# Six plain up-projections, sums in ten steps, and two products' pools exchanged, in a hybrid decoder's inference step

## The chip, the cores and the metric

The kernel runs on one core of a Trainium2 chip. A core has a matrix engine (TensorE, with its weight loads listed apart as PEld), a vector engine (VectorE, DVE in the trace), an activation engine (ScalarE, ACT), a general engine (GpSimd, POOL) and queues that start DMA transfers (SyncE, SP). Each engine executes its own instructions in a fixed order and waits on semaphores for the others. The metric is the device time of one launch in microseconds; less is better. Executions of the same kernel differ by some tenths of a per cent.

## The reference

Two layers (DEPTH = 2) of a decoder trunk are applied to 1024 prompt tokens and to 8 x 4 sample tokens. In each layer three kinds of heads mix the tokens, a projection and a layer norm follow, and then a gated convolutional feed-forward part, the one that the change touches:

```python
def _conv_ffn(x, conv0, w_up, conv_w, conv_b, w_down):
    t_ = x.shape[1]
    u = x @ w_up
    buf = jnp.concatenate([conv0.astype(u.dtype), u], axis=1)
    c = conv_b + sum(conv_w[j] * buf[:, j:j + t_] for j in range(CONV_W))
    a, b = jnp.split(c, 2, axis=-1)
    return (jax.nn.gelu(a) * b) @ w_down, buf[:, -(CONV_W - 1):]
...
        f, cv = _conv_ffn(x, s_conv[l], ffn_up[l], ffn_conv_w[l], ffn_conv_b[l], ffn_down[l])
        x = _layer_norm(ALPHA * x + f, ln2_g[l], ln2_b[l])
```

D_MODEL is 1024, D_FF 2816, CONV_W 3; everything is float32.

## The kernel before

Activations lie with channels on the 128 partitions and tokens along the free axis. The 1056 tokens are cut into three blocks n = 0, 1, 2 of 384, 384 and 288 columns; block 2 holds the 32 sample tokens first. To keep float32 accuracy in fast matmuls every operand is split into a high and a low part (`split`: a cast on ScalarE, the difference on GpSimd, or on VectorE where said), and each product is three matmuls: high x high, high x low and low x high (`mm3`, recorded at line 140).

The feed-forward part runs over NJ = 22 steps j, one for 128 gate channels and the 128 value channels that belong to them. A step makes the two up-projections u (8 k-tiles of 128 input channels each), the three-tap convolution (`conv_start`, line 1437, on ScalarE, then `taps`, line 1433, on VectorE), the gate (`up_gate`: GELU on ScalarE, the product on VectorE at line 1467, then the split), and hands the result to the down-projection. Steps are taken in pairs (j, j + 1). In the middle of step j the function `between` runs the down-projection of the pair before, `downs(j - 2, ...)`: for two halves, three blocks and four output tiles, 24 groups of six matmuls, each group into one PSUM tile, which VectorE then adds to an accumulator `acc[n][m]` in SBUF. The third argument `group` of `downs` counts the pairs: 0 for the first. In group 0 the accumulator isn't read but set, and the residual ALPHA * x goes in, with its high part first (it frees the PSUM tile) and its low part after it: two VectorE instructions per group of matmuls (line 1664). In later groups it is one addition (line 1660).

There are two ways to make a step. `up_first` (step 0) and `up_plain` (steps 1 to 3) multiply directly: per half i of the step (gate, value) and block n, 8 k-tiles x 3 matmuls. `up` (steps 4 to 21) treats blocks 0 and 1, the two halves of the channels and the two halves of k as a 2 x 2 product in Winograd's form: seven products of four k-tiles for eight (into tiles named pa, pg, pb, pc, pf, pd and pe), with weight sums s1 to s4 made on VectorE (lines 1602 to 1605) and sums of activations q1 to q4; block 2 is done directly there, in tiles p0 and p1 (both `p` in the trace). The results are put together on VectorE with additions from PSUM (lines 1596, 1610, 1616, 1617, 1623, 1624, 1633).

The sums of activations q1 to q4 must exist before step 4. The generator `sums` makes them, split into high and low parts: for each of four k-tiles t3 = x1[1] upper minus lower quarter (differences on GpSimd), then t2 and t4 (differences on VectorE), eight VectorE and five GpSimd instructions per k. Last come the differences that overwrite the lower quarter of x1[1] in place, on GpSimd for even k and VectorE for odd. Differences live in buffers d that share a ring of six (tag `u`) with the up-projections. `up_plain` calls `then(j, i, n)` after each group, and where that place stands in `times`, the generator does its next piece: one k after each of the first four places, the whole in-place part after the fifth.

PSUM has eight tiles of a bank: three in pool `pg`, five in pool `pd`. Plain groups take `pd` tiles for n = 0, 1 and `pg` tiles for n = 2 (`bank`); in `up` p0, p1 and the second product (p2, named pg) are in `pg`, the others and all down groups in `pd`. A tile that is taken again makes TensorE wait until its last reader is done.

The order of TensorE is the order in which the program writes the matmuls. The other engines' orders come from the compiler's scheduler, which goes by program order and by the times of a simulated run, so an instruction can be moved ahead of one that is not ready in that simulation. On the chip each engine then keeps that order.

Of the kernel before, what the change touches and what calls it, by code (L numbers as in the profile page):

```python
# [10 lines left out]
F32 = mybir.dt.float32  # L11
# [3 lines left out]
ALU = mybir.AluOpType  # L15
# [3 lines left out]
P = 128  # L19
# [11 lines left out]
ALPHA = (2 * DEPTH) ** 0.25  # L31
# [138 lines left out]
def step_kernel(ctx: ExitStack, tc: tile.TileContext, xT, wA, wB, wO, wU, wD, pp, pb, lora, bg, bgk, shT, cvT, srw, sgl, srt,  # L170
# [12 lines left out]
    pg = pool("pg", 3, PSUM)  # L183
# [137 lines left out]
    for l in range(depth):  # L321
# [1151 lines left out]
        def sums():  # L1473


            (h0, l0, _), (h1, l1, _) = x1[:2]
            t2, t3, t4 = ([jp.tile([P, 4, 384], F32R, tag="tq", name=f"{n}{p}", bufs=6) for p in "hl"] for n in ("t2", "t3", "t4"))

            def x(n, k):
                return [t[:, k].bitcast(F32) for t in x1[n][:2]]  # L1480

            qs = [(h0[:, 0:4], l0[:, 0:4]), (h0[:, 4:8], l0[:, 4:8]), (h1[:, 4:8], l1[:, 4:8]), (h1[:, 0:4], l1[:, 0:4]), t2, t3, t4]
            yield qs

            def new():
                return fp.tile([P, 386], F32, tag="u", name="d", bufs=6)[:, 0:384]

            def two(h, lo, raw, e):
                A.copy(h, raw)
                e.tensor_tensor(lo, raw, h.bitcast(F32), ALU.subtract)  # L1490

            def apart(e, a, b):

                d, f = new(), new()
                e.tensor_tensor(d, a[0], b[0], ALU.subtract)
                e.tensor_tensor(f, a[1], b[1], ALU.subtract)
                e.tensor_tensor(d, d, f, ALU.add)
                return d

            def minus(e, a, d):  # L1500

                e.tensor_tensor(d, a[0], d, ALU.subtract)
                e.tensor_tensor(d, d, a[1], ALU.add)
            for k in range(4):
                d = apart(G, x(1, k + 4), x(1, k))
                two(t3[0][:, k], t3[1][:, k], d, G)
                d = apart(V, x(1, k), x(0, k))
                minus(V, x(1, k + 4), d)
                two(t2[0][:, k], t2[1][:, k], d, G)
                f = new()  # L1510
                V.tensor_tensor(f, x(0, k + 4)[0], d, ALU.subtract)
                V.tensor_tensor(f, f, x(0, k + 4)[1], ALU.add)
                two(t4[0][:, k], t4[1][:, k], f, V)
                yield
            for k in range(4):
                d = apart(V if k % 2 else G, x(1, k), x(0, k))
                two(h1[:, k], l1[:, k], d, V)
            yield

        def product(ps, w, x, first=True, last=True):  # L1520

# [3 lines left out]
        def bank(n, name):  # L1525
            return (pg.tile([P, 512], F32, tag="g", name=name) if n == 2 else pd.tile([P, 512], F32, tag="d", name=name))[:, :NB[n][1]]
# [30 lines left out]
        def up_plain(j, between, then):  # L1557

            hs, cs = [], []
            for i in range(2):  # L1560
                t = j + i * NJ
                w, prev = [whole(wu(t, half), f"wU{t}") for half in range(2)], None
                for n in range(3):
                    c, prev = plain(t, i, n, w, prev)
                    cs.append(c)
                    if i:
                        hs.append(up_gate((cs[n], c), n))
                    then(j, i, n)
                if i == 0:
                    between()  # L1570
            return hs

        def up(j, qs, late=False, between=lambda: None):


            b11, b21, b22, q1, q2, q3, q4 = qs
            t0, t1 = j, j + NJ
            x2 = [(x1[2][0][:, 0:4], x1[2][1][:, 0:4]), (x1[2][0][:, 4:8], x1[2][1][:, 4:8])]
            r11, r12, r21, r22 = (raw_piece(wu(t, half), f"wU{t}") for t in (t0, t1) for half in range(2))
            pa = bank(0, "pa")  # L1580
            w = piece(r11, "a11")
            product(pa, w, b11)
            u22 = new_u()
            A.copy(u22[:, 2:386], pa)
            if not late:
                p0, p1 = bank(2, "p0"), bank(2, "p1")
                product(p0, w, x2[0], True, False)
            w = piece(r12, "a12")
            if not late:
                product(p0, w, x2[1], False, True)  # L1590
                c20, u20 = conv_samples(t0, 0, p0)
            p2 = pg.tile([P, 512], F32, tag="g", name="pg")[:, :384]
            product(p2, w, b21)
            u11 = new_u()
            v11, v22 = u11[:, 2:386], u22[:, 2:386]
            V.tensor_tensor(v11, v22, p2, ALU.add)
            c11 = conv_prompt(t0, 0, u11, v11, True)
            if not late:
                product(p1, piece(r21, "a21"), x2[0], True, False)

            s1 = wf.tile([P, 512], F32, tag="wr", name="s1r", bufs=FR)
            V.tensor_tensor(s1, r21, r22, ALU.add)
            V.tensor_tensor(r21, r11, r21, ALU.subtract)
            V.tensor_tensor(r11, s1, r11, ALU.subtract)
            V.tensor_tensor(r12, r12, r11, ALU.subtract)
            pb_ = bank(0, "pb")
            product(pb_, piece(r11, "s2"), q2)
            u12 = new_u()
            v12 = u12[:, 2:386]
            V.tensor_tensor(v12, v22, pb_, ALU.add)  # L1610
            between()
            p5 = bank(0, "pc")
            product(p5, piece(s1, "s1"), q1)
            p7 = bank(0, "pf")
            product(p7, piece(r21, "s3"), q3)
            V.tensor_tensor(v22, v12, p7, ALU.add)
            V.tensor_tensor(v12, v12, p5, ALU.add)
            p4 = bank(0, "pd")
            w = piece(r22, "a22")
            product(p4, w, q4)  # L1620
            u21 = new_u()
            v21 = u21[:, 2:386]
            V.tensor_tensor(v21, v22, p4, ALU.add)
            V.tensor_tensor(v22, v22, p5, ALU.add)
            halo(u22, 1, u21)
            hs = [up_gate((c11, conv_prompt(t1, 1, u21, v21, True)), 0)]
            if not late:
                product(p1, w, x2[1], False, True)
                c21, u2 = conv_samples(t1, 1, p1)
                conv_rest(t1, c21, u2, u22)  # L1630
            p3 = bank(0, "pe")
            product(p3, piece(r12, "s4"), b22)
            V.tensor_tensor(v12, v12, p3, ALU.add)  # L1633
            halo(u12, 1, u11)
            c12 = conv_prompt(t0, 0, u12, v12)
            hs.append(up_gate((c12, conv_prompt(t1, 1, u22, v22)), 1))
            if late:
                for t, half, p in ((t0, 0, 0), (t0, 1, 0), (t1, 0, 1), (t1, 1, 1)):
                    if half == 0:
                        ps = bank(2, f"pu{t}")  # L1640
                    product(ps, whole(wu(t, half), f"wU{t}"), x2[half], half == 0, half == 1)
                    if half:
                        c, u = conv_samples(t, p, ps)
                        conv_rest(t, c, u, (u12, u22)[p])
                        if p:
                            c21 = c
                        else:
                            c20 = c
            else:
                conv_rest(t0, c20, u20, u12)  # L1650
            hs.append(up_gate((c20, c21), 2))
            return hs

        def down(m, n, group, hs, ws):
            ps = pd.tile([P, 512], F32, tag="d", name="pd")[:, :NB[n][1]]
            for i, (h, w) in enumerate(zip(hs, ws)):
                mm3(ps, *w, *h[n], i == 0, i == len(hs) - 1)
            a = acc[n][m]
            if group:
                V.tensor_tensor(a, a, ps, ALU.add)  # L1660
            else:

                for x, y in zip(x1[n][:2], (ps, a)):
                    V.scalar_tensor_tensor(a, x[:, m].bitcast(F32), ALPHA, y, ALU.mult, ALU.add)

        def downs(j, hs, group):
            for half in range(2):
# [5 lines left out]

        make = sums()
        qs = next(make)
        times = ((1, 0, 2), (1, 1, 2), (2, 0, 2), (2, 1, 2), (3, 1, 1))

        def then(*at):
            if at in times:
# [2 lines left out]
        for j in range(0, NJ - 2, 2):  # L1682

            def between():
                if j:
                    downs(j - 2, hs, j // 2 - 1)
            if j == 0:
                a = up_first()
            elif j < 4:
                a = up_plain(j, between, then)  # L1690
            else:
                a = up(j, qs, between=between)
            hs = [a, up(j + 1, qs) if j >= 4 else up_plain(j + 1, lambda: None, then)]

        xs = [None] * 3

# [213 lines left out]
```

## Time and profile before

| | us |
|---|---|
| median of 3 runs (lowest, highest) | 3405.08 (3397.25, 3408.31) |
| the profiled execution's own time | 3395.68 |
| its span, first to last instruction | 3393.9 |

The mean granted TensorE clock of the profiled execution is 0.945 of full speed. Layer 0's feed-forward part takes about 883 to 1660 us of the span, layer 1's about 2580 to 3370 us. In the profile's rows a line is that of the kernel or of a helper, `out<-in` names the tiles, a bracket gives the idle time before an instruction and what ended it, and a matmul's duration (0.34 us for 384 columns) overlaps the next one's, so that the distance of starts is what counts. A few records of matmuls can be missing.

### The profile page before, as it was taken

The numbers are of one execution on the slowest core, as the hardware profiler recorded it, in microseconds if no ns is written. First come the engines' busy times: TensorE is split into PE (matmuls) and PEld (weight loads), VectorE is DVE, ScalarE is ACT, GpSimd is POOL, SyncE is SP. The second block draws the span as 40 slices with busy tenths as digits, with TensorE's granted clock in tenths as the row PEclk, the third lists the DMA queues.
The fourth block names the chain that finished last, engine by engine and source line by source line (L and its number), as shares of the span: only waits on it lengthen the run. The fifth ranks groups of instructions, "written<-read, shape, count | busy, mean of one in ns | idle before, by whom it ended". The sixth has DMA issues, their size and how long they took to land. (4 is left out here: it accounts for less than half of the span.)

```text
span 3393.9 us, 59056 instructions
## 1 busy us (share of the span) xinstructions
PE 3103.4 (91%) x21618; PEld 2868.3 (85%) x21618; DVE 2374.4 (70%) x5085; ACT 1577.6 (46%) x3635; POOL 1575.1 (46%) x1512
## 2 busy tenths in 40 slices
PE   8889999998889999999788899998998899999995
PEld 8778887777889999999687787876778899999994
DVE  3586764566797777777857667644667977777778
ACT  6754432654534334434586534325545334344346
POOL 5542222144655555545675422221346555455556
PEclk9989999988999999999898899998989899999997
DMA  7443223443301111111264432233433011111111
GB/s 242 147 130 83 70 68 121 120 131 104 90 26 44 56 43 46 47 54 54 96 193 142 115 78 68 65 118 113 129 114 90 25 44 54 41 51 47 54 53 66
DMA packets 245566, 291.14 MB, mean 86 GB/s; under 512 B 76620, under 2 KB 158316, under 8 KB 245276
## 3 DMA queue, kind: packets, MB, share of 16 engines
q1 hardware_dynamic: 225004, 274.08, 26.8%
q10 hardware_dynamic: 20272, 13.29, 1.6%
q8 instruction: 170, 2.79, 0.3%
q14 instruction: 120, 0.98, 0.1%
HBM read 228.85 MB, written 58.43 MB: 85 GB/s over the span
## 5 line engine op out<-in xcount | busy, mean ns | idle before, releaser
L1433 DVE SCALAR_TENSOR_TENSOR c<-u,ppt,c 128x32 f32<-128x32 f32 (+3 forms) x704 | 514.2, 762 | 71.3 <-ACT c L1437 65.9
L197 POOL TENSOR_TENSOR wil<-wir,wih 128x512 fp32r<-128x512 f32 (+1 forms) x264 | 368.7, 1407 | 253.9 <-ACT wih L197 228.8
L140 PE MATMUL gt<-wih,xh 128*128 128x320 f32 (+1 forms) x1008 | 347.5, 346 | 4.6 <-DVE mx L404 4.6
L140 PE MATMUL gt<-wil,xh 128*128 128x320 f32 (+1 forms) x1008 | 322.2, 321 | 5.8 <-POOL wil L197 5.8
L1660 DVE TENSOR_TENSOR acc<-acc,pd 128x384 f32<-128x384 f32 (+1 forms) x480 | 239.4, 517 | 112.7 <-PE pd L140 110.2
L140 PE MATMUL gt<-wih,xl 128*128 128x320 f32 x896 | 286.0, 319 | 0.0
L197 ACT CAST wih<-wir 128x512 fp32r<-128x512 f32 (+1 forms) x296 | 184.5, 636 | 131.4 <-PE po L140 57.5
L140 PE MATMUL pa<-xh,wih 128*128 128x384 f32 (+1 forms) x576 | 208.7, 362 | 29.3 <-ACT wih L197 12.4
L653 DVE TENSOR_TENSOR tm<-U,N 96x60 f32<-96x60 f32 (+24 forms) x558 | 175.1, 314 | 81.2 <-DMA N<-gd 66.1
L140 PEld LDWEIGHTS gt<-wih,xh 128*128 128x128 f32 (+1 forms) x1008 | 192.1, 191 | 42.4 <-issue 24.6
L140 PE MATMUL pa<-xh,wil 128*128 128x384 f32 (+1 forms) x576 | 197.5, 343 | 12.5 <-POOL wil L197 12.5
L140 PEld LDWEIGHTS gt<-wil,xh 128*128 128x128 f32 (+1 forms) x1008 | 193.6, 192 | 10.1 <-POOL wil L197 8.6
L140 PE MATMUL pa<-xl,wih 128*128 128x384 f32 (+1 forms) x576 | 195.7, 340 | 0.8 <-POOL xl L197 0.8
L140 PEld LDWEIGHTS gt<-wih,xl 128*128 128x128 f32 x896 | 177.2, 198 | 0.0
L655 DVE TENSOR_TENSOR U<-U,tm 96x60 f32<-96x60 f32 (+24 forms) x558 | 164.6, 295 | 16.3 <-DMA tokd<-ev 0.3
L197 POOL TENSOR_TENSOR hl<-c,hh 128x384 fp32r<-128x384 f32 x132 | 139.4, 1066 | 53.0 <-ACT hh L197 53.0
L140 PEld LDWEIGHTS pa<-xh,wih 128*128 128x128 f32 x576 | 117.3, 204 | 44.0 <-ACT wih L197 13.6
L140 PE MATMUL po<-yh,wih 128*128 128x384 f32 (+1 forms) x384 | 136.1, 354 | 12.1 <-DVE ac L1349 10.2
L1437 ACT ACTIVATE c<-u,ppt 128x384 f32<-128x384 f32 x144 | 101.8, 708 | 85.3 <-DVE u L1633 39.9
L140 PEld LDWEIGHTS pa<-xh,wil 128*128 128x128 f32 x576 | 117.0, 203 | 16.6 <-POOL wil L197 16.6
L140 PE MATMUL po<-yl,wih 128*128 128x384 f32 (+1 forms) x384 | 128.1, 334 | 0.0
L140 PE MATMUL po<-yh,wil 128*128 128x384 f32 (+1 forms) x384 | 128.0, 333 | 0.0
(967 smaller groups left out, 10199.1 us busy)
## 6 DMA issues: line engine op xcount, KB each, us to landing
wir<-in_wA_dram SPq DMA_DIRECT2D x144, 256.0 KB
wir<-in_wO_dram SPq DMA_DIRECT2D x96, 256.0 KB
wir<-in_wB_dram SPq DMA_DIRECT2D x56, 320.0 KB
tokd<-ev SPq DMA_DIRECT2D x112, 160.0 KB
x<-rkvd SPq DMA_DIRECT2D x16, 576.0 KB
tk<-tokd SPq DMA_DIRECT2D x16, 480.0 KB
rkvd<-mx SPq DMA_DIRECT2D x36, 192.0 KB
tk<-tokd SPq DMA_DIRECT2D x16, 400.0 KB
```

Of the source, the lines that this page charges most:

```text
L140: self.order(self.engine.matmul(out, lhsT, rhs, start=start, stop=stop), cols, 4 if rhs.dtype == F32 else 1)
L197: return A.copy(dst_h, src), (le or G).tensor_tensor(dst_l, src, dst_h.bitcast(F32), ALU.subtract)
L653: V.tensor_tensor(tm, U[:, 0:nr, i:i + 1].to_broadcast([4 * ns, nr, 31 - i]), N[:, i:i + 1, i + 1:32].to_broadcast([4 * ns, nr, 31 - i]), ...
L655: V.tensor_tensor(U[:, 0:nr, i + 1:32], U[:, 0:nr, i + 1:32], tm, ALU.add)
L1433: V.scalar_tensor_tensor(cv[..., o:], uu[..., tap + o:tap + w], pc(PP_CV + 4 * t + tap), cv[..., o:], ALU.mult, ALU.add)
L1437: A.activation(c, src, AF.Identity, scale=pc(PP_CV + 4 * t + 2), bias=pc(PP_CV + 4 * t + 3))
L1660: V.tensor_tensor(a, a, ps, ALU.add)
```

## The change

Steps 4 and 5 are made by `up_plain` instead of `up`. The generator `sums` stops ten times instead of five: after t3 of each k, after t2 and t4 of each k, and twice in the in-place part; the ten places in `times` now run from step 1 to step 5. The residual's low part is added in group 1 for block 0, in group 0 for block 1 and in group 2 for block 2; its high part stays in group 0. In `up`, the second product p2 takes a tile of pool `pd` and the third, pb, a tile of pool `pg`.

```diff
@@ sums @@
             for k in range(4):
                 d = apart(G, x(1, k + 4), x(1, k))
                 two(t3[0][:, k], t3[1][:, k], d, G)
+                yield
                 d = apart(V, x(1, k), x(0, k))
...
                 two(h1[:, k], l1[:, k], d, V)
-            yield
+                if k % 2:
+                    yield
@@ up @@
-            p2 = pg.tile([P, 512], F32, tag="g", name="pg")[:, :384]
+            p2 = bank(0, "pg")
...
-            pb_ = bank(0, "pb")
+            pb_ = pg.tile([P, 512], F32, tag="g", name="pb")[:, :384]
@@ down @@
             if group:
                 V.tensor_tensor(a, a, ps, ALU.add)
-            else:
-
-                for x, y in zip(x1[n][:2], (ps, a)):
-                    V.scalar_tensor_tensor(a, x[:, m].bitcast(F32), ALPHA, y, ALU.mult, ALU.add)
+
+            for i, x in enumerate(x1[n][:2]):
+                if group == (i and (1, 0, 2)[n]):
+                    V.scalar_tensor_tensor(a, x[:, m].bitcast(F32), ALPHA, a if group or i else ps, ALU.mult, ALU.add)
@@ the loop over steps @@
-        times = ((1, 0, 2), (1, 1, 2), (2, 0, 2), (2, 1, 2), (3, 1, 1))
+        times = ((1, 0, 1), (1, 1, 1), (2, 0, 0), (2, 1, 2), (3, 0, 1), (3, 1, 1), (4, 0, 0), (4, 1, 2), (5, 1, 1), (5, 1, 2))
...
-            elif j < 4:
+            elif j < 6:
                 a = up_plain(j, between, then)
             else:
                 a = up(j, qs, between=between)
-            hs = [a, up(j + 1, qs) if j >= 4 else up_plain(j + 1, lambda: None, then)]
+            hs = [a, up(j + 1, qs) if j >= 6 else up_plain(j + 1, lambda: None, then)]
```

## The prediction

> **What bounds the kernel now.** I read the page's busy times first, then the table of what TensorE waited for over the whole run.
>
> ```profile
> PE 3103.4 (91%) x21618; PEld 2868.3 (85%) x21618; DVE 2374.4 (70%) x5085; ACT 1577.6 (46%) x3635; POOL 1575.1 (46%) x1512
> ```
>
> TensorE is the bound, so time is won only where it idles or runs slowly. Its waits (us in total, times, longest):
>
> ```profile
> PE pd L140 <- DVE u L1610: 15.3, 16, 2.0
> ...
> PE pd L140 <- ACT c L1437: 11.9, 4, 4.6
> PE p L140 <- ACT c L1437: 10.7, 2, 5.4
> ...
> PE pd L140 <- DVE acc L1664: 8.3, 2, 4.2
> ```
>
> Four of these lie where the diff works, all for a PSUM tile that VectorE or ScalarE has not emptied: 11.9 + 8.3 us in the first down-projection block, 10.7 us at p1 of the first Winograd step, 15.3 us in sixteen small waits for line 1610. They are counted over two layers.
>
> Next, stretches of time (columns: length, then busy time and count of PE, PEld, DVE, ACT, POOL, then the granted clock).
>
> ```profile
> 945.00:990.00 45.00, 35.34 (x193) 33.09 (x192) 43.74 (x75) 12.75 (x31) 23.46 (x21) 0.85 0.13 42
> 975.00:1020.00 45.00, 45.00 (x283) 44.80 (x282) 40.84 (x65) 14.81 (x38) 23.08 (x21) 1.00 0.06 18
> 1025.00:1050.00 25.00, 19.63 (x112) 19.31 (x111) 19.25 (x32) 9.78 (x26) 15.02 (x16) 0.86 0.16 44
> 1100.00:1125.00 25.00, 24.13 (x147) 23.60 (x146) 18.18 (x34) 8.40 (x18) 12.50 (x12) 1.00 0.25 75
> 2642.00:2687.00 45.00, 34.38 (x184) 32.54 (x183) 43.71 (x72) 12.43 (x30) 23.67 (x22) 0.81 0.13 40
> 2725.00:2750.00 25.00, 19.62 (x106) 19.30 (x105) 17.89 (x31) 9.92 (x25) 13.92 (x15) 0.86 0.21 60
> ```
>
> The second row is undisturbed: 283 matmuls, 0.159 us each on average. The first block (945 and 2642) holds 193 and 184, so it loses 90 x 0.159 = 14.3 and 99 x 0.159 = 15.7 us, together 30.0 us. The stretches around p1 hold 112 and 106 where 157 would fit: 7.2 + 8.1 = 15.3 us. Both exceed the waits themselves because the granted clock falls to 0.81 to 0.86 there. VectorE is 97% busy in the first block (43.7 of 45): it is the engine that is late.
>
> **The change, part by part.**
>
> *Six plain up-projections.* Steps 4 and 5 do eight products of four k-tiles instead of seven: 4 x 3 = 12 more 384-column matmuls each, 48 over two steps and two layers.
>
> ```profile
> 896.60 0.34 PE L140 MATMUL pu<-x1h,wUwh 128*128 128x384 f32 x1
> ...
> 897.46 0.34 PE L140 MATMUL pu<-x1h,wUwl 128*128 128x384 f32 x1
> ```
>
> Five starts in 0.86 us are 0.173 us each: **+8.3 us**, certain, since TensorE has no slack to hide it. The loads by DMA stay four per step. ScalarE and GpSimd are spared four of eight weight splits, VectorE four weight sums and seven additions from PSUM; I count that as nothing, since none of them is the bound in a steady step.
>
> *Sums in ten steps, and the low parts.* Rows: VectorE's, ScalarE's and GpSimd's work on the temporaries d in the 42 us around the first block's start,
>
> ```profile
> 923.00:965.00 42.00, 20.59 (x23) 4.10 (x9) 16.05 (x14) 0.88 0.08 26
> ```
>
> then that on the accumulators (VectorE alone) in the first block and in the next, which TensorE runs through without a wait:
>
> ```profile
> 947.00:992.00 45.00, 25.55 (x48) 0.00 (x0) 0.00 (x0) 0.85 0.13 42
> 1038.00:1062.00 24.00, 11.96 (x24) 0.00 (x0) 0.00 (x0) 1.00 0.23 67
> ```
>
> Before, 23 VectorE instructions (nearly three k, eight each) run there at 20.59/23 = 0.90 us. After, only the second half of the first k belongs ahead of the block: 8 x 0.90 = 7.2 us, so 13.4 us go. The step placed after the first group of step 2 has GpSimd work only; GpSimd falls from 14 instructions to about nine. In the block itself 48 evictions (25.55 us) become 24 + 8, or 17.0 us, against 22.9 us of TensorE (16 groups of six matmuls at 1.04 us, 8 at 0.78 with 288 columns). Are the waits then gone? The row
>
> ```profile
> 947.67 0.34 PE L140 MATMUL pd<-hh,wD0wh 128*128 128x384 f32 x1
> ```
>
> is the block's first matmul; ScalarE's reads of the two tiles that the groups before it hold:
>
> ```profile
> 953.95 0.68 ACT L1437 ACTIVATE c<-pu,ppt 128x384 f32<-128x384 f32 x1
> ...
> 958.08 0.68 ACT L1437 ACTIVATE c<-pu,ppt 128x384 f32<-128x384 f32 x1
> ```
>
> and on VectorE the first eviction of the block:
>
> ```profile
> 964.66 0.54 DVE L1664 SCALAR_TENSOR_TENSOR acc<-x1h,pd 128x384 f32<-128x384 f32 x1
> ```
>
> Two of the five pd tiles hold up-projections, so groups four and five, at 950.8 and 951.9, need the two ScalarE instructions, which ended 954.6 and 958.8; group six, at 952.9, needs line 1664, which ended 965.2. ScalarE runs in order and stood behind VectorE. With the second k's 7.2 us gone the first two move to about 947.4 and 951.6; with 13.4 us gone the third moves to 951.8. All three are just met. One thing is new in ScalarE's order: the cast of the step after the first group of step 2 waits for three differences on GpSimd (16.05/14 = 1.15 us each, 3.4 us), and the reads of the following tiles stand behind it. So I keep 2 us of loss per layer (bounds 0, and 7.5, half of today's loss). **Gain 30.0 - 4 = 26.0 us**, bounds 15 and 30.0. The low parts that move: eight in each of the next two blocks at about 0.54 us, 11.96 + 4.3 = 16.3 us of VectorE in a 22.9 us block, hidden by its slack there. They read no PSUM, so they free no tile later, except that the next eviction stands behind them.
>
> The second wait, at p1: ScalarE's order,
>
> ```profile
> 1028.03 0.20 ACT L1450 COPY u<-cvt 128x16 f32<-128x16 f32 x1 [2.41 <-DVE x1l L1490]
> ...
> 1031.30 0.51 ACT L1489 CAST x1h<-d 128x384 fp32r<-128x384 f32 x1 [2.45 <-DVE d L1497]
> ...
> 1032.06 0.61 ACT L1437 ACTIVATE c<-pu,ppt 128x288 f32<-128x288 f32 x1
> ```
>
> and TensorE's:
>
> ```profile
> 1032.72 0.61 PE L140 MATMUL p<-x1h,a21wh 128*128 128x288 f32 x1 [5.37 <-ACT c L1437]
> ```
>
> p1 waits for the tile of the last plain group, whose convolution start stands behind two ScalarE instructions that wait 4.9 us for the in-place sums (one for a u buffer that a difference holds, one for the difference). After, half of these sums are issued behind that group, and it ends near 1027.8. With the pools exchanged the tile is wanted by pb, not p1: 1032.72 - 5.37 + 12 x 0.13 = 1028.9. So the wait goes with 1 us to spare; I keep 1 us per layer (bounds 0 and the whole). **Gain 15.3 - 2 = 13.3 us**, bounds 0 and 15.3. The later half of the in-place sums is not wanted until the down block is past.
>
> *Pools exchanged.* One steady Winograd step, TensorE and then VectorE:
>
> ```profile
> 1174.21 0.34 PE L140 MATMUL pd<-hh,wD7wl 128*128 128x384 f32 x1
> 1175.41 0.44 PE L140 MATMUL pd<-hh,wD6wh 128*128 128x384 f32 x1 [0.86 <-DVE u L1610]
> ```
>
> ```profile
> 1174.81 0.55 DVE L1610 TENSOR_TENSOR u<-u,pb 128x384 f32<-128x384 f32 x1
> 1175.28 3.08 DVE L1660 TENSOR_TENSOR acc<-acc,pd 128x384 f32<-128x384 f32 x6
> ```
>
> The fifth down group wants pb's tile and is delayed 1.03 us (1174.38 to 1175.41). With pb in the other pool the sixth group is the first to wait, at 1175.43, for the first eviction, which ends 1175.28 + 3.08/6 = 1175.8: 0.4 us. So 0.6 us x 16 = **9.6 us gained**, bounds 0 (the wait only changes its name) and 15.3. Do the exchanged tiles find room? Last reads of the step before, on ScalarE and VectorE, then TensorE's starts:
>
> ```profile
> 1161.35 0.61 ACT L1437 ACTIVATE c<-p,ppt 128x288 f32<-128x288 f32 x1
> ```
>
> ```profile
> 1162.89 0.55 DVE L1633 TENSOR_TENSOR u<-u,pe 128x384 f32<-128x384 f32 x1
> ```
>
> ```profile
> 1164.19 0.34 PE L140 MATMUL pg<-x1h,a12wh 128*128 128x384 f32 x1
> ...
> 1167.86 0.33 PE L140 MATMUL pb<-t2h,s2wh 128*128 128x384 f32 x1
> ```
>
> p2 (named pg in the trace) starts at 1164.19, after the last of the previous step's four pd tiles was freed (1163.4); pb starts 5.9 us after the old p1 was freed (1162.0). Neither adds a wait.
>
> **A rule beside the rows.** The Trainium skill, "TensorE: Matmul & The Clock Gate", section "Part 1: The HAM clock gate", says the clock halves after an idle window of about 3.4 us and needs as long busy to return. The trace agrees: in the stretches with waits of 4.2 to 5.4 us the clock is 0.81 to 0.86; the one from 1100 on, with a wait for line 1610 (mean 15.3/16 = 0.96 us) in it, keeps 1.00. By that rule a remaining wait of 2 us costs only itself; were the clock to fall as today (30.0 lost for 11.9 + 8.3 idle), it would cost half more, 2 us over both layers.
>
> **Sum.** 8.3 - 26.0 - 13.3 - 9.6 = -40.6 us. Against the profiled execution (3395.7 us, span 3393.9) that is 3355.1; that execution is 9.4 us below the median of the runs, 3405.1, so for the median I forecast 3405.1 - 40.6 = **3364.5 us**.
>
> **The rivals.**
> *Half stays* (VectorE remains late through the first blocks because the compiler orders its queue otherwise than I assume, and the exchange only renames its wait): 8.3 - 15.0 - 7.7 - 0 = -14.4, 3390.7 us. For it: every deadline above is met by about 1 us or less. Against it: VectorE has 13 us less to do ahead of the block.
> *The waits move on* to the second down block and to step 6: nothing won on the two large terms, 8.3 - 9.6 = -1.3, 3404 us. This is also the case that the ten steps don't spread anything. Against it: in the second row of the stretches (975 to 1020) sums run beside two plain groups, VectorE has 40.8 of 45 us, and TensorE loses nothing.
> *Slower: the low parts bind the two later blocks.* The row that prices it:
>
> ```profile
> L1664 DVE SCALAR_TENSOR_TENSOR acc<-x1l,acc x48: 444/545/1560, 965.2 to 2689.3; 128x384 f32<-128x384 f32 x32, 128x288 f32<-128x288 f32 x16
> ```
>
> Their longest is 1.56 us, 0.54 is the middle. Blocks one and two then take 11.96 + 8 x 1.56 = 24.4 us of VectorE against 22.9; from (22.9 - 11.96)/8 = 1.37 us each VectorE decides. That is 1.5 us x 4 blocks; such contended times also keep the sums as late as now, so nothing else is won and the exchange is eaten by the late VectorE: 8.3 + 6.0 = +14.3, 3419 us. The Trainium skill, "SBUF — State Buffer", section "SBUF: two separate sides", says that a VectorE instruction with two SBUF inputs and a GpSimd instruction lock each other out for the whole instruction; by that rule the low parts, moved to where GpSimd is busier, would often be the long ones. The trace agrees in kind (444 to 1560 ns for one form), but the median stays short.
>
> **How the numbers follow.** Chances: forecast 0.66, half stays 0.20, waits move on 0.09, slower 0.05. Low end: all bounds at their best, 8.3 - 30.0 - 15.3 - 15.3 = -52.3, which is 3353 from the median and 3343 from the profiled execution; I take 3346. High end: "half stays" with a little room, 3393; what lies beyond it has 0.14. A measurement here tells 0.3% (10.2 us) from no change: faster 0.84 (forecast, and nine tenths of "half stays"), same 0.11, slower 0.05.
>
> **What would show it.** In the changed profile TensorE's waits for line 1437 and for the residual's line inside the first down block should be at most about 2 us a layer, with the granted clock at 1.00 there; the wait at the first Winograd step should be gone or under 1 us, now at step 6; the waits for line 1610 should be replaced by waits of some 0.4 us for the accumulator; 48 more matmuls should stand in the count. Wrong I would be if VectorE were still over 95% busy in that block with TensorE waiting, or if a new PSUM wait stood at p2 or pb.

## The result, and the profile after

| | us, median (lowest, highest) | runs |
|---|---|---|
| before | 3395.70 (3385.99, 3408.31) | 10 |
| after | 3372.76 (3358.63, 3388.74) | 10 |

The ratio is 0.9933 (95% interval 0.9908 to 0.9958): the change wins 22.9 us, 0.67%. The profiled execution of after took 3360.67 us, 12 us less than its median; of the 35.6 us between the two profiled spans, 13.0 lie ahead of and between the feed-forward parts, where the code is the same. So I compare stretches of the feed-forward parts: from the first matmul of wU1 to the end of the last down matmul, both layers, 1497.06 us before (748.16 + 748.90) and 1475.16 after (738.30 + 736.86). That is 21.9 us less, in accord with the medians.

The page's busy times, then two rows of TensorE's waits over the whole run (us in total, times, longest):

```profile
PE 3094.9 (92%) x21666; PEld 2861.9 (85%) x21666; DVE 2348.3 (70%) x5041; ACT 1573.0 (47%) x3631; POOL 1555.5 (46%) x1496
```

```profile
PE pd L140 <- DVE acc L1662: 16.6, 18, 4.1
...
PE pd L140 <- DVE acc L1666: 5.6, 4, 1.7
```

The 48 added matmuls are there (21666 against 21618). The waits for line 1610 (15.3 us) and the 10.7 us at p1 are gone. Line 1662 is the old 1660, line 1666 the residual's. Of the 16.6 us, 7.1 stand in the last down blocks of the two layers (4.14 and 2.99), where line 1660 cost 8.3 before (3.93 and 4.40), and 4.4 in step 4's; nearly all of the others are about 0.3 us. Now the first down block in stretches like the prediction's, layer 0 and layer 1 (length; busy time and count of PE, PEld, DVE, ACT, POOL; granted clock):

```profile
936.00:981.00 45.00, 41.71 (x251) 40.74 (x250) 33.75 (x57) 14.08 (x36) 18.53 (x17) 0.96 0.13 42
2619.00:2664.00 45.00, 41.66 (x248) 40.69 (x247) 33.61 (x56) 14.27 (x36) 18.37 (x17) 0.96 0.13 40
```

251 and 248 matmuls stand where 193 and 184 stood and 283 would fit, and VectorE's load fell from 43.7 to 33.7 of 45 us. Most of the loss is gone, but not all. To see where each microsecond went I took the lengths of the down blocks from TensorE's timeline (start of a block's first matmul to start of the next other matmul; us, layer 0 / layer 1). The third column is the distance from the first Winograd step's pa to its down block, 11.02 when nothing waits:

| | block of step 2 | of step 4 | of step 6 | first pa to its block |
|---|---|---|---|---|
| before | 37.70 / 39.23 | 23.36 / 23.20 | 24.45 / 24.56 | 18.39 / 19.18 (step 4) |
| after | 28.80 / 29.02 | 25.75 / 25.82 | 27.32 / 27.23 | 11.78 / 11.70 (step 6) |

The seven blocks after these take 172.48 + 171.59 us before and 169.19 + 166.89 after. By this: first block -19.1 us, the stretch from pa -14.1, the seven later blocks -8.0, the 48 matmuls +8.3, and two losses that I had not counted, **+5.0 in the block of step 4 and +5.5 in that of step 6**. Together -22.4.

What is left in the first block is seen in three timelines, TensorE's waits first (start, duration, idle time before and what ended it):

```profile
943.82 0.45 PE L140 MATMUL pd<-hh,wD0wh 128*128 128x384 f32 x1 [0.48 <-ACT c L1437]
...
946.23 0.44 PE L140 MATMUL pd<-hh,wD0wh 128*128 128x384 f32 x1 [1.10 <-DVE acc L1666]
...
949.26 0.62 PE L140 MATMUL pd<-hh,wD0wh 128*128 128x384 f32 x1 [1.72 <-DVE acc L1666]
949.68 0.52 PE L140 MATMUL pd<-hl,wD0wh 128*128 128x384 f32 x1
```

ScalarE:

```profile
938.93 0.68 ACT L1437 ACTIVATE c<-pu,ppt 128x384 f32<-128x384 f32 x1
...
942.30 0.53 ACT L1466 ACTIVATE c<-c 128x384 f32<-128x384 f32 x1 [2.51 <-DVE c L1433]
942.73 0.46 ACT L1539 COPY u<-pu 128x384 f32<-128x384 f32 x1
943.09 0.68 ACT L1437 ACTIVATE c<-pu,ppt 128x384 f32<-128x384 f32 x1
...
945.74 0.52 ACT L1466 ACTIVATE c<-c 128x384 f32<-128x384 f32 x1 [0.96 <-DVE c L1433]
```

VectorE:

```profile
939.64 2.57 DVE L1433 SCALAR_TENSOR_TENSOR c<-u,ppt,c 128x383 f32<-128x383 f32 x2 [1.45 <-ACT c L1437]
943.80 1.91 DVE L1433 SCALAR_TENSOR_TENSOR c<-u,ppt,c 128x384 f32<-128x384 f32 x2 [1.59 <-ACT c L1437]
945.63 0.54 DVE L1666 SCALAR_TENSOR_TENSOR acc<-x1h,pd 128x384 f32<-128x384 f32 x1
947.66 1.08 DVE L1433 SCALAR_TENSOR_TENSOR c<-u,ppt,c 128x32 f32<-128x32 f32 x3 [1.49 <-ACT c L1437]
```

Read the first two together. ScalarE starts one group's convolution at 938.93; VectorE makes the taps; ScalarE's next instruction is that group's GELU (1466), which waits 2.51 us for the taps, and only behind it stand the copy and the convolution start that read the next group's PSUM tile. VectorE meanwhile waits for ScalarE, 1.59 us. The two hand one chain back and forth, each idle while the other works: a **relay**. It looks no longer like a lack of VectorE time but like an order on ScalarE; run 6 tests this.

The block of step 4 has one wait, 2.18 us for the eviction 1662, and the same relay ahead of it (a row of TensorE and one of ScalarE):

```profile
1022.41 0.44 PE L140 MATMUL pd<-hh,wD2wh 128*128 128x384 f32 x1 [2.18 <-DVE acc L1662]
```

```profile
1014.99 0.53 ACT L1466 ACTIVATE c<-c 128x384 f32<-128x384 f32 x1 [2.53 <-DVE c L1433]
```

In step 6 three engines have to be read side by side. TensorE:

```profile
1083.49 0.44 PE L140 MATMUL pb<-t2h,s2wh 128*128 128x384 f32 x1 [0.48 <-ACT c L1437]
...
1087.51 0.45 PE L140 MATMUL pd<-hh,wD5wh 128*128 128x384 f32 x1 [1.10 <-ACT wD5wh L197]
...
1089.08 0.52 PE L140 MATMUL pd<-hh,wD5wl 128*128 128x384 f32 x1 [0.96 <-POOL wD5wl L197]
```

ScalarE:

```profile
1082.07 0.51 ACT L1489 CAST x1h<-d 128x384 fp32r<-128x384 f32 x1 [5.13 <-DVE d L1497]
...
1082.84 0.60 ACT L1437 ACTIVATE c<-pu,ppt 128x288 f32<-128x288 f32 x1
...
1086.84 0.61 ACT L197 CAST wD5wh<-wD5r 128x512 fp32r<-128x512 f32 x1
```

VectorE, and below it GpSimd:

```profile
1077.36 1.36 DVE L1495 TENSOR_TENSOR d<-x1h,x1h 128x384 f32<-128x384 f32 x1
1078.64 1.36 DVE L1496 TENSOR_TENSOR d<-x1l,x1l 128x384 f32<-128x384 f32 x1
1079.93 1.64 DVE L1433 SCALAR_TENSOR_TENSOR c<-u,ppt,c 128x384 f32<-128x384 f32 x1
1081.49 0.55 DVE L1497 TENSOR_TENSOR d<-d 128x384 f32<-128x384 f32 x1
```

```profile
1078.26 1.33 POOL L1497 TENSOR_TENSOR d<-d 128x384 f32<-128x384 f32 x1
1079.55 1.60 POOL L197 TENSOR_TENSOR wD4wl<-wD4r,wD4wh 128x512 fp32r<-128x512 f32 x1
1082.74 0.48 POOL L1454 COPY cvt<-u 128x16 f32<-128x16 f32 x1 [1.58 <-ACT u L1451]
```

ScalarE stood still for 5.13 us at the cast of an in-place difference that VectorE had not made yet. Behind that cast were the read of the last plain tile and, further on, wD5's cast; so the down block, which needs wD5, paused twice. The two stops in the generator's in-place part did not put half of its four casts behind the last plain group: three stand ahead of the read at 1082.84 (at 1072.34, 1074.46 and 1082.07) and one behind it (1083.32), as before the change.

### The profile page after: what moved, and what is told of

Its sections match the earlier page's. It is cut to its first block, busy times and chain, and to the rows that moved or that the text cites. A ratio compares the mean times of both kernels' runs of the same rounds, so it can differ in the third digit from the quotient of the medians.

```text
span 3358.3 us, 59010 instructions
## 1 busy us (share of the span) xinstructions
PE 3094.9 (92%) x21666; PEld 2861.9 (85%) x21666; DVE 2348.3 (70%) x5041; ACT 1573.0 (47%) x3631; POOL 1555.5 (46%) x1496
## 5 line engine op out<-in xcount | busy, mean ns | idle before, releaser
L1437 ACT ACTIVATE c<-u,ppt 128x384 f32<-128x384 f32 x128 | 90.5, 708 | 75.4 <-DVE u L1635 35.3
```

The lines of the kernel that those rows point to most:

```text
L1437: A.activation(c, src, AF.Identity, scale=pc(PP_CV + 4 * t + 2), bias=pc(PP_CV + 4 * t + 3))
```

## The experiments

Each run is compared by stretches as above, since whole times of single runs differ by more than 10 us in parts that none of these edits touches. Blocks are layer 0 / layer 1 in us, "total" is the two feed-forward parts (before 1497.1, after 1475.2).

**1. The exchange of pools alone**, on the kernel before:

```diff
-            p2 = pg.tile([P, 512], F32, tag="g", name="pg")[:, :384]
+            p2 = bank(0, "pg")
-            pb_ = bank(0, "pb")
+            pb_ = pg.tile([P, 512], F32, tag="g", name="pb")[:, :384]
```

> The kernel before with the two products' pools exchanged and nothing else. Theory (the wait of the fifth down group is pb's tile in the five-tile pool): the 16 waits of 15.3 us for the line that reads pb go, waits of about 0.3 us for the accumulator take their place, and a steady down block falls from 24.4 to 24.5 us to about 23.9 us, 8 to 10 us over both layers; the wait at p1 of step 4 moves to pb and falls from 5.4 to about 3.7 us, because pb is wanted 1.6 us later. First block unchanged at 37.7 and 39.2 us. Rival (the exchange only helped together with the sums' new places): steady blocks stay at 24.4 us, waiting for the accumulator instead.

Total 1489.4, -7.6; one execution took 3384.95 us beside 3413.13 of before. The waits for line 1610 are gone, eight for the accumulator (4.6 us) stand from 1060 to 1600. The eight blocks from step 6 on take 387.6 us (193.7 + 193.9) against 393.1. The wait at p1 moved to pb:

```profile
1025.68 0.45 PE L140 MATMUL pb<-t2h,s2wh 128*128 128x384 f32 x1 [3.85 <-ACT c L1437]
```

The third tile that the step takes from pool `pg`, in order of use, is the one the last plain group held (p0, p2, p1 before; p0, p1, pb here). Here that is pb, whose turn comes 1.6 us later (12 matmuls of p1 at 0.13 us). So the exchange helps at both places.

**2. The change with the old pools:**

> The changed kernel with the pools as before. Theory: the first block stays at 28.8 to 29.0 us and the second at 25.8, the steady blocks go back to about 24.4 us with waits of 0.9 us for the line that reads pb, and at p1 of step 6 a wait of about 2 us per layer comes back (the tile is freed 9.5 us after the last plain matmul, p1 wants it 7.4 us after). Rival: the exchange also made the first block shorter, which would be over 30 us here.

Total 1487.2, +12.1 against after, 10.2 of it in layer 0. In layer 1 the seven blocks from step 8 on take 171.4 us against 166.9: 0.64 us each, beside the 0.6 of the prediction. p1 waits 1.99 / 1.95 us. But step 6's block is 24.17 / 24.10 here: with TensorE already held at p1, wD5 comes nearly in time (0.76 us of wait). So the whole of layer 1 is only 1.9 us longer. In layer 0, four later blocks take 25.7 to 27.4 us; in three of them the wait for the line that reads pb is 2.02 us instead of 0.9, and the granted clock is 0.50 for 3.41 us behind it. Before had one such wait in layer 0 (its block took 25.48), without the fall of the clock. Most of the 12.1 is this, and not what the exchange steadily brings.

**3. The change with the residual's low parts all in group 0:**

```diff
-                if group == (i and (1, 0, 2)[n]):
+                if group == 0:
```

> The changed kernel with all low parts of the residual back in the first block (48 VectorE instructions there, 24 in the two later blocks). Theory (the sums ahead of the block were what made it late, the low parts matter little): first block 29 to 31.5 us for 28.8 to 29.0, second block at most 0.5 us shorter than 25.8. Rival (the number of instructions in the block was the cause): first block 34 us or more.

Total 1474.6 (738.50 + 736.08), 0.6 less than after: no difference. First block 29.10 / 30.51, step 4's 25.10 / 25.16. What the first block gains from moving them, the next gives back.

**4. Six plain steps alone**, on the kernel before, with the in-place part at the end of the plain steps as there:

```diff
-        times = ((1, 0, 2), (1, 1, 2), (2, 0, 2), (2, 1, 2), (3, 1, 1))
+        times = ((1, 0, 2), (1, 1, 2), (2, 0, 2), (2, 1, 2), (5, 1, 1))
...
-            elif j < 4:
+            elif j < 6:
...
-            hs = [a, up(j + 1, qs) if j >= 4 else up_plain(j + 1, lambda: None, then)]
+            hs = [a, up(j + 1, qs) if j >= 6 else up_plain(j + 1, lambda: None, then)]
```

> The kernel before with six plain steps, sums in five pieces at their old places but the in-place piece after the second group of step 5, old pools, low parts in the first block. Theory: the first block is as long as before, 37.7 and 39.2 us, since nothing ahead of it moved; a down block in step 4 now lies among plain groups and costs about 2.5 us more than 23.3; the wait at p1, now at step 6, is under 3 us, because VectorE has had two more steps to catch up and the in-place piece is all that is left. Rival (the plain steps themselves give the gain): first block below 33 us.

Total 1494.3 (745.41 + 748.85), -2.8. First block 37.70 / 39.34, as before. From pa to the block 11.02 / 11.05: no wait at all, 15.5 us won for the 8.3 of the added matmuls. Step 4's block is 23.88 / 23.89 and step 6's 24.11 / 24.06, where the expectation had step 4's longer: so **the losses in both blocks of the change are not the plain steps' own**. Step 4's comes with the sums placed ahead of it; step 6's with how late the in-place sums are, since these stand ahead of that block here too. Why the wait is gone shows in the read of the last plain tile and in p1:

```profile
1094.27 0.61 ACT L1437 ACTIVATE c<-pu,ppt 128x288 f32<-128x288 f32 x1
```

```profile
1095.11 0.29 PE L140 MATMUL p<-x1h,a21wh 128*128 128x288 f32 x1
```

pa starts at 1087.78, so the read ends 7.1 us after it, and p1 comes at 7.3. Before, with pa at 1019.85, the read ended at 12.8; after, with pa at 1073.93, at 9.5. In all three the same casts stand ahead of the read, and what differs is when VectorE starts its first difference of the in-place part (before, after, this run):

```profile
1017.66 0.55 DVE L1495 TENSOR_TENSOR d<-x1h,x1h 128x384 f32<-128x384 f32 x1
```

```profile
1068.37 0.55 DVE L1495 TENSOR_TENSOR d<-x1h,x1h 128x384 f32<-128x384 f32 x1
```

```profile
1079.80 0.55 DVE L1495 TENSOR_TENSOR d<-x1h,x1h 128x384 f32<-128x384 f32 x1
```

That is 2.2, 5.6 and 8.0 us ahead of pa, and the read ends 15.0 to 15.1 us later each time. The same 15.0 to 15.1 us stand in all eleven kernels that make the in-place part ahead of the first Winograd step (all but runs 7 and 11), whether it is cut in two or not.

**5. The change with five stops**, a whole k each, at the later place of each pair:

```diff
-                yield
...
-                if k % 2:
-                    yield
+            yield
...
+        times = ((1, 1, 1), (2, 1, 2), (3, 1, 1), (4, 1, 2), (5, 1, 1))
```

> The changed kernel with the sums in five steps again: each k whole, at the later of its two places, and the in-place part whole after the second group of step 5. Theory (what matters is where VectorE's sums lie, not into how many pieces they are cut; the first halves are GpSimd's): first block 28 to 29 us, second 25 to 26, step 6's 26.5 to 27.5, the feed-forward stretches within 1.5 us of 738.3 and 736.9. Rival (the cut into ten is what helps): first block over 31 us, or step 6's first Winograd tiles waiting 2 us or more.

Total 1479.0, +3.8. First block 26.52 / 26.04, step 4's 30.42 / 29.26, step 6's 25.43 / 24.18, pb waits 2.38. The blocks missed what I expected (no change there), and the longer wait at pb is one of the two signs that the rival named: the in-place part starts 3.6 us ahead of pa here instead of 5.6. On the whole the finer cut, with the places that go with it, is worth 3.8 us; mostly it moves the loss between blocks.

**6. The relay.** The change, with the GELU of a plain group ordered behind the convolution start of the second half's group in the same step:

```diff
-        def up_gate(cs, n):
+        def up_gate(cs, n, prev=None):
 
-            A.activation(cs[0], cs[0], AF.Gelu_apprx_tanh)
+            TE.after(A.activation(cs[0], cs[0], AF.Gelu_apprx_tanh), prev)
...
-                        hs.append(up_gate((cs[n], c), n))
+                        hs.append(up_gate((cs[n], c), n, started[0]))
```

`started[0]` is the last instruction that `conv_start` issued for a PSUM tile.

> The changed kernel where a plain step's GELU for a block may not stand ahead of the second half's read of that block's PSUM tile on ScalarE. Theory (what is left in the first two blocks is a relay: ScalarE's GELU waits for VectorE's taps and the next tile's reads stand behind it): first block 24 to 26 us instead of 28.8 and 29.0, second 23.5 to 24.5 instead of 25.8. Rival (VectorE is simply late from the sums ahead of the block): first block 28 us or more, second 25 or more.

Total 1458.3 (728.48 + 729.83), **-16.9 us**. First block 24.96 / 25.35, step 4's 23.24 / 23.25, step 6's 24.38 / 24.38, no wait at pb. ScalarE in the first block (the edit moves these lines down by two):

```profile
951.40 0.47 ACT L1541 COPY u<-pu 128x384 f32<-128x384 f32 x1
951.77 0.68 ACT L1439 ACTIVATE c<-pu,ppt 128x384 f32<-128x384 f32 x1
...
952.53 0.49 ACT L1541 COPY u<-pu 128x384 f32<-128x384 f32 x1
952.90 0.69 ACT L1439 ACTIVATE c<-pu,ppt 128x384 f32<-128x384 f32 x1
```

The two reads stand 1.13 us apart; in after they were 4.16 (938.93 to 943.09). No engine does less work, and the loss of step 4's block is gone entirely. The relay is shown to be needed for that loss, for most of step 6's, and for 3.8 / 3.7 us of the 5.6 / 5.8 by which the first block exceeds 23.2, the length without a wait. For the rest of it TensorE still waits for evictions (0.82 + 0.43 us in layer 0).

**7. The in-place sums behind the down block of step 6**, the rest as in the change:

```diff
-        times = ((1, 0, 1), (1, 1, 1), (2, 0, 0), (2, 1, 2), (3, 0, 1), (3, 1, 1), (4, 0, 0), (4, 1, 2), (5, 1, 1), (5, 1, 2))
+        times = ((1, 0, 1), (1, 1, 1), (2, 0, 0), (2, 1, 2), (3, 0, 1), (3, 1, 1), (4, 0, 0), (4, 1, 2))
...
                     downs(j - 2, hs, j // 2 - 1)
+                if j == 6:
+                    next(make), next(make)
```

> The changed kernel with the in-place sums issued behind the down groups of step 6 instead of in step 5. Theory (a cast of the in-place sums waits 5.1 us for VectorE and the cast of the down weights wD5 stands behind it): step 6's block 24 to 25 us instead of 27.3 and 27.2, no wait at pb; 2 to 3 us less per layer. Rival (wD5's weights are late by their load): the wait for wD5 stays at about 1 us for each part and the block at 27 us. A third case: the sums are late for the product that follows the block, and a new wait stands there.

Total 1465.7, -9.5. Step 6's block 24.02 / 23.71, from pa to it 11.02 in both layers, the other two blocks unchanged (28.73 / 28.87 and 25.62 / 25.61). So without the in-place sums ahead of it the loss in step 6 is gone, and nothing waits for them later. By runs 4 and 6 they do that harm only when they are late.

**8. The sums clear of the first block**, all ten places later:

```diff
+        times = ((2, 1, 0), (2, 1, 2), (3, 0, 0), (3, 0, 2), (3, 1, 0), (3, 1, 1), (4, 1, 0), (4, 1, 1), (5, 1, 1), (5, 1, 2))
```

> The changed kernel with the sums' ten places moved so that VectorE's part of no k lies right ahead of a down block: first k after step 2's block, two more in step 3, the last in the second half of step 4. Theory (each VectorE part right ahead of a block costs that block 2 to 3 us): first block 25 to 27 us instead of 28.8 and 29.0, second 24 instead of 25.8, with the loss of the last steps unchanged. Rival (the relay between ScalarE and VectorE is all that is left): first block 28 us or more. Risk: VectorE gets behind in step 3, and the second block is longer than 26 us.

Total 1483.8, +8.6. The first block is undisturbed, 23.20 / 23.20, and step 4's takes 34.22 / 34.30. Its waits in layer 0:

```profile
PE pd L140 <- ACT c L1437: 3.2, 2, 2.5
PE pd L140 <- DVE acc L1662: 1.8, 2, 1.2
```

The lateness moved whole, and more came with it: the case that the expectation named as the risk. At pb TensorE waits 2.13 / 2.10 us. The first block has the GELU between the two reads here too (reads at 938.09 and 940.96, 2.9 us apart, the block from 942.96 on), and loses nothing: so the relay alone costs no time, it passes on a lateness that the sums bring.

**9. The same with the GELU order of run 6:**

> The changed kernel with the sums' places clear of the blocks (first block 23.2, second 34.2 and 34.3 us) and the GELU order on top. Theory (the second block's loss there was VectorE's backlog from three k in step 3, reached through ScalarE's order): first block stays at 23.2, second falls to 26 to 30 us. Rival (all of it was the order): second under 24.5 us, and the feed-forward stretches under 727 us, which would be the best version.

Total 1469.9. First block 23.20 / 23.19, step 4's 29.53 / 29.50, step 6's 27.10 / 27.14. The relay explains 4.7 of the 11 us that step 4's block lost in run 8; the rest stays, I think because VectorE has that many sums there. That step 6's block is no shorter than in the change, though there is no wait at pb, also shows that the order alone does not free it: the in-place part starts 6.5 us ahead of pa, in run 6 it was 8.0.

**10. The GELU order alone, on the kernel before:**

> The kernel before with the GELU order alone. Theory (before, VectorE's sums made the first block late, and ScalarE's order adds to it): first block 30 to 35 us instead of 37.7 and 39.2. Rival A (the order on ScalarE was the whole cause, so that the new places were not needed): first block under 27 us. Rival B (only the sums count): 37 us or more. The wait at p1 of step 4 stays within 1 us of 5.4 in the theory.

Total 1492.6 (745.03 + 747.61). First block 39.03 / 39.89, no shorter, as rival B had it: where VectorE itself is late, as it was before, ScalarE's order is worth nothing to that block. One row of TensorE's waits in it (line 1666 is the residual's there):

```profile
PE pd L140 <- DVE acc L1666: 7.6, 1, 7.6
```

The wait at p1 did fall, from 5.4 to 2.30 / 2.42, which I had not expected.

**11. Runs 6 and 7 together:**

> The changed kernel with both: GELU not ahead of the reads, and the in-place sums behind the down groups of step 6. If the two losses are separate, the feed-forward stretches come to 727 to 730 us each (738.3 and 736.9 for the changed kernel, 748.2 and 748.9 before), that is 38 to 42 us below the kernel before over both layers, a ratio of 0.987 to 0.990. If the second loss is already gone with the first (no wait at pb there), it is no better than 728.5 and 729.8.

Total 1457.7 (727.79 + 729.88), -39.4 against before and only 0.6 less than run 6: with the relay gone VectorE is early enough that the in-place sums cost step 6 little. Median 3366.89 us (3349.84 to 3378.17, 6 runs) beside 3399.86 (3388.62 to 3425.38, 11 runs), ratio 0.9894 (0.9854 to 0.9935). It is the shortest of all by the stretches; its interval overlaps the change's, so by whole times the two are not told apart.

## Why the prediction was right, and where it was wrong

The forecast case came true in kind, and the time (3372.8) lies 8 us above 3364.5 and inside the range of 3346 to 3393. That is partly luck: the forecast stood on a median of 3405.1 from three runs, and ten gave 3395.7. Against a gain of 40.6 us the runs gave 22.9. By its steps:

- **Six plain steps, +8.3.** The 48 matmuls are counted in the profile. Run 4 shows what the step buys, which the prediction credited to the sums and to the pools: the wait at the first Winograd step goes with the plain steps alone.
- **The wait at p1, gain 13.3.** Measured 14.1 (6.6 + 7.5): right in size. Its working was wrong: "half of these sums are issued behind that group, and it ends near 1027.8" would be 8.0 us after pa, and it was 9.5. The cut put nothing behind the read that hadn't been there before: three of the four casts stayed ahead of it, and the in-place part took its 15 us as in every other kernel (run 4). What was won there came from its earlier start. The margin came from pb: its turn is 8.9 us after pa, hence the 0.48 us that were left, inside the 1 us that I had kept.
- **The first block, gain 26.0.** Measured 19.1. The mis-sized term is the rest: I kept 2 us a layer, and it was 5.6 / 5.8. I looked for it in GpSimd's differences; run 6 shows it in the GELU's place on ScalarE. Of the three deadlines "met by about 1 us or less", the first had 3.4 us by the prediction's own numbers (947.4 for 950.8) and was met; ScalarE's second read came 0.48 us late; and the eviction, which I put at 951.8 for group six wanted at 952.9, let TensorE wait 1.10 us, the one after it 1.72. So the first sign, at most about 2 us of such waits a layer at a clock of 1.00, was missed: 3.3 us at 0.96. The rows quoted for the reads had the answer between them: they stood 4.1 us apart before the change too, 953.95 and 958.08, with a waiting GELU in the middle, and I took that distance as due to the sums alone.

```profile
957.29 0.52 ACT L1466 ACTIVATE c<-c 128x384 f32<-128x384 f32 x1 [2.47 <-DVE c L1433]
```

- **The low parts, cost nothing.** Right (run 3), and nothing of the slower rival was seen. But they gave nothing on the whole either: fewer evictions made the first block 1.8 us shorter over both layers, and the next one 1.3 us longer.
- **Pools exchanged, gain 9.6.** The step is right: 0.6 us a block forecast, 0.64 in run 2 and 0.67 in the seven late blocks of layer 1 (171.59 - 166.89 = 4.7). Seven blocks a layer gave 8.0; step 6's block, in which the same wait went, is under the next point. What the exchange is worth in sum is less sure: run 1 puts it at 7.6 us in the kernel before, run 2 at 1.9 us in the change's undisturbed layer, where step 6's block loses 3.1 and the stretch from pa gains 1.6.
- **What the prediction left out, +10.5.** It followed the sums out of the first block, but not to the blocks that they were put ahead of: the step that failed is the claim from the stretch 975 to 1020 that sums beside plain groups cost TensorE nothing. Ahead of the blocks of steps 4 and 6 they cost 5.0 and 5.5 us. Runs 4, 6 and 7 show this: without sums ahead of it step 4's block is 23.9 (run 4) and step 6's 24.0 and 23.7 (run 7), and with the sums there but without the relay they are 23.2 and 24.4 (run 6). The rival "the waits move on" had this mechanism, at too high a price for all of it: a third of what was won moved on (10.5 of 33.2).
- **The clock.** That "a remaining wait of 2 us costs only itself" held for the 2.18 us in step 4's block. It failed in the first block and in step 6, where shorter waits followed each other (last section).

## What to carry to other kernels

When work is moved off a late engine, look at the places it is moved to with the same care as at the place it leaves: the queue that is read behind it, on every engine that hands it on. An instruction that waits for another engine should not stand, in an in-order queue, ahead of one that frees a PSUM tile; reordering that (run 6) was worth 16.9 us, three quarters of what the whole change won, with no work removed. It was worth nothing in a block where the engine waited for was itself late (run 10), and there was nothing to win where the work arrived early enough (run 8). Cutting work finer (run 5) or spreading it (run 3) is worth little by itself, since the lateness goes along.

## What was not expected of the hardware

**The clock fell without a long wait.** Three stretches of after (columns as above): with the 1.72 us that end the waits of the first block (0.48 and 1.10 us went before), with the single 2.18 us in step 4's, and behind the 1.10 and 0.96 us in step 6's.

```profile
948.00:952.00 4.00, 2.74 (x9) 2.75 (x10) 3.97 (x10) 0.44 (x1) 0.62 (x3) 0.67 0.42 125
...
1020.00:1024.00 4.00, 1.82 (x11) 1.60 (x10) 3.65 (x9) 0.76 (x2) 1.30 (x3) 1.00 0.40 131
...
1089.00:1093.00 4.00, 3.92 (x13) 3.92 (x14) 3.15 (x8) 1.83 (x4) 0.93 (x4) 0.57 0.23 68
```

After the two waits of about 1 us in step 6, starts of matmuls stood 0.32 us apart instead of 0.17 for 3.5 us (1089.08 to 1092.6), about 11 matmuls or 1.6 us lost; after one wait of 2.18 us the clock stayed at 1.00. The traces show what decides. The granted clock is 1.00 or 0.50 in them, and every stretch of either but the last of a trace lasts a multiple of 3.41 us. Cut along these boundaries, the places of the first and second row look so:

```profile
945.94:949.35 3.41, 1.40 (x7) 1.09 (x7) 1.92 (x6) 1.69 (x5) 2.68 (x4) 1.00 0.36 83
949.35:952.77 3.42, 3.42 (x11) 3.42 (x12) 3.35 (x8) 0.44 (x1) 0.00 (x0) 0.50 0.20 71
1017.63:1021.04 3.41, 2.60 (x15) 2.21 (x13) 1.92 (x4) 1.89 (x5) 3.41 (x5) 1.00 0.12 32
1021.04:1024.46 3.42, 2.05 (x12) 2.06 (x13) 3.42 (x9) 0.45 (x1) 0.26 (x1) 1.00 0.35 121
```

The 2.18 us lie on both sides of the boundary at 1021.04 and leave TensorE 2.60 and 2.05 us busy; the shorter waits in one stretch leave 1.40, and the next 3.41 us run at 0.50. In the feed-forward parts of all 13 traces, up to the last down block, each of the 40 falls follows a stretch with TensorE busy for at most 0.53 of it by this view, and each stretch at full clock below 0.47 is followed by a fall. So what counts is how much idle time one such stretch holds, about half of it, and the same wait can cost the clock or not by where it lies. The Trainium skill, "TensorE: Matmul & The Clock Gate", section "Part 1: The HAM clock gate", gives an idle window of about 3.4 us and as long to return: the time to return agrees (3.5 us), but in the change's first block and step 6, where the clock fell, no single idle stretch was longer than 1.72 us.

**VectorE and GpSimd took turns.** In the rows of step 6 above, VectorE's differences and taps took 1.36 to 1.64 us and GpSimd's 1.33 to 1.60 as long as both had work, and starts on each stood 1.3 us apart; as soon as GpSimd had none (from 1081.2), the same kind of difference on VectorE (1497) took 0.55. So a VectorE instruction of the sums, which the prediction counted at about 0.9 us, takes 1.4 in such a place; that is part of why VectorE ran late there. The Trainium skill, "SBUF — State Buffer", section "SBUF: two separate sides", says that a VectorE instruction with two SBUF inputs and a GpSimd instruction that reads SBUF lock each other out for the whole instruction; these rows agree in kind.
